# One core, a decoder layer on a hand-ordered TensorE stream: prepared blocks ahead of other late work, two closing products exchanged, the first quads' sums on VectorE, and a quarter of the k-tiles later where a stage begins

## The chip, the cores and the metric

The kernel runs on one core of a Trainium2 chip. The metric is the device time of one execution in microseconds (us), lower is better; a time is the median of several executions. The profile is one execution taken by the hardware profiler. Engines are named as in its rows: PE is TensorE (matmul), PEld its weight loads, DVE is VectorE, ACT is ScalarE, POOL is GpSimd, SP is SyncE, which issues most DMAs. L355 is line 355 of the kernel.

## The reference

One decoder layer on 256 tokens of width 2048 in float32: a half SwiGLU, a mixer, a second half SwiGLU, a final norm.

```python
x = x + 0.5 * swiglu(rmsnorm(x), ffn1_w_gate, ffn1_w_up, ffn1_w_down)      # 2048 -> 5632 -> 2048
x = x + hybrid_mixer(rmsnorm(x), w_in, ...)      # one projection w_in, attention, gated MLP, merge, w_out
x = x + 0.5 * swiglu(rmsnorm(x), ffn2_w_gate, ffn2_w_up, ffn2_w_down)
return rmsnorm(x, final_norm)

swiglu(h)       = (silu(h @ w_gate) * (h @ w_up)) @ w_down
hybrid_mixer(h) : proj = h @ w_in  -> q, k, v (3 x 1536), u, vs (1536), g_att, g_sg (2048)
                  y_att = attention(q, k, v) @ w_att_out;  y_sg = (gelu(u) * spatial(vs)) @ w_sg_out
                  merged = sigmoid(g_att) * y_att + sigmoid(g_sg) * y_sg;  return merged @ w_out
```

## The kernel before

All tokens stay in the core's memory; the weights stream through once. Every float32 product is made of three fp32r products: an operand is split into a high part (rounded, a copy by ACT) and a low part (the rest, a subtraction by DVE), and high x high, high x low and low x high are summed in PSUM. For the tokens these are `xhi`/`xlo` (h of the FFN: `hA`/`hB`; merged: `mhi`/`mlo`), for the weights `wh`/`wl`.

**Steps.** The work of PE is a list of steps (`steps`, made by `lay_out`). An ordinary step ("n") is two k-tiles of 128 rows by 512 columns of one weight; its unit `raw` is 512 KB, loaded by SP (L250), split by ACT (L348, `wh<-raw`) and DVE (L349, `wl<-raw`; all DVE instructions carry L66, a metering wrapper), and used by 12 matmuls (L355). `wh` and `wl` are rings of nine k-tiles. A function `advance` splits some three steps ahead of PE where the ring has room. A gemm has eight or fewer such steps (q = 0 to 7), one per two k-tiles.

**Quads.** For pairs of neighbouring gemms (512 columns each) some k-tiles are multiplied in Strassen's way, with seven block products p1 to p7 in place of eight: `nq` is 2 or 3 k-tile pairs (a row 128x1024 or 128x1536). The weight's four blocks B11, B21 (first gemm), B12, B22 (second) are loaded by `load_block` as `quads` (blocks 0 to 3). `prepare` makes from them f = B12+B22, t2 = f-B11, t1 = t2-B22, t4 = t2-B21, in this order (`todo`); p6 uses t2, p7 f, p5 t1, p4 t4. In rows `sum` or `part` is where t2 and t4 go, `quads` where f and t1 go. For the FFN quads f was made by the DMA itself: POOL loads block 3 onto block 2 with an accumulating DMA (L292). For the others DVE adds. Blocks of the next quad load when a product has freed their room (`FREES`: p5, p2, p7, p3). Token sums for the quads are `fx`, `fy`, `fh...`, `uTA`/`uTB`.

**Banks.** A quad has four PSUM banks: q11, q21 of its first gemm, q12, x_ of its second (`qd_0` to `qd_3` in rows). p1, p6, p7, p5 run in x_; after p5, DVE writes q12 = x_ + part (L414, a row `qd<-qd,quads`, `qd<-qd,part` or `qd<-qd,vs`), and from then on everything of the second gemm adds to q12 and x_. p3 goes to q12, p4 to q21, p2 to q11. `opening` puts p1, p6, p7 among the last steps of the gemms before, `closing` puts p5, p3, p4, p2 among the first steps of the quad's own.

**Order.** The first element of `group` is how many gemms are laid out together, the second a key that sorts their steps. `PAIR`, used where a stage's tokens come in quarters (four k-tiles each, c = 0 to 3), keeps the last two steps of both gemms (last quarter) for the end. It is used for the first pair of w_in, of w_out, of ffn2's gate, and of parts of the down product, which is cut into three parts (`PARTS`) of k-tiles as the FFN's columns get ready.

The rest is a planner at the time the program is built: `now[0]` is the step's time, `at(i, fn)` calls fn at a time, `extra(wait, slack, cost, fn)` puts work on a heap that `work_off` empties when the metered DVE load allows or the slack is over, `prepare_ready` prepares quads in `started` when their blocks are loaded, and `prepare_for` forces what a form about to be split needs. `move_in` loads the first four blocks of a home (a set of buffers for quads: two FFNs, gates, merge) at a given time. The engines then run their queues in program order, and semaphores do the rest.

Of the kernel before, what the change touches and what calls it, by code (L numbers as in the profile page):

```python
# [71 lines left out]
def layer(ctx: ExitStack, tc: tile.TileContext, a, out):  # L72
# [57 lines left out]
    quads = []  # L130
# [9 lines left out]
    slots = []  # L140

    def closing(count):
        return zip((1, 2, 3, 5) if count > 9 else (1, 2, 3, 4), ("p5", "p3", "p4", "p2"))

    def opening(count):
        return zip((5, 3, 1) if count > 9 else (4, 2, 1), ("p1", "p6", "p7"))
# [1 line left out]
    def lay_out():  # L148
        i, count = 0, 0
        while i < len(gemms):  # L150
            g = gemms[i]
            size, stage = g["group"]
            quad = g["quad"]
            taken = range(quad["k0"] // 2, quad["k0"] // 2 + quad["nq"]) if quad else ()
            order = [(p, q) for p in range(size) for q in range(gemms[i + p]["nk"] // 2) if q not in taken]
            if stage:
                order.sort(key=lambda s: stage(*s, gemms[i + s[0]]["nk"] // 2))
            new = [("n", (gemms[i + p], q // 2, q % 2)) for p, q in order]
            if quad:
                nq = quad["nq"]  # L160
                quad["gemms"] = gemms[i], gemms[i + 1]
                quad["loaded"], quad["split"] = {}, set()
                quad["todo"] = ["t2", "t1", "t4"] if quad["home"] in homes else ["f", "t2", "t1", "t4"]
                for k, form in opening(count):
                    steps.insert(len(steps) - k, ("s", (quad, form)))
                for k, form in reversed(list(closing(len(order)))):
                    new.insert(k, ("s", (quad, form)))
                quads.append(quad)
                for h in quad["gemms"]:
                    h["left"] = [3 * (h["nk"] - nq)] * NT  # L170
                gemms[i + 1]["left"][1] += 9 * nq
            steps.extend(new)
            count = len(order) if size > 1 else 16
            i += size
        t, pos = -1.0, 0
        for kind, s in steps:
            width = 2 if kind == "n" else s[0]["nq"]
            t += 1 if kind == "n" else width / 4
            ends.append(t)
            slots.append([(pos + q) % RING for q in range(width)])  # L180
            pos += width
            if kind == "n":
                hus.append(s)
                s[0]["steps"] += 1
            else:
                s[0]["gemms"][s[1] in ("p3", "p5", "p6", "p7", "p1")]["steps"] += 1
# [13 lines left out]
        return found  # L200


    PAIR = (2, lambda p, q, m: q >= m - 2)
    BOTH = (2, None)
    FIRST = (4, lambda p, q, m: 4 if q >= 4 else 3 if q >= 2 else 2 if p == 3 else q)

# [8 lines left out]

        heapq.heappush(extras, (now[0] + slack, next(counter), now[0] + wait, cost, fn))

    def work_off():
        DVE.load = max(0.0, DVE.load - TICK * (now[0] - now[1]))
        now[1] = now[0]  # L220
        while True:
            ready = [e for e in extras if e[2] <= now[0]]
            if not ready:
                return
            e = min(ready)
            if e[0] > now[0] and DVE.load + e[3] > FULL:
                return
            extras.remove(e)
            heapq.heapify(extras)
            e[4]()  # L230

    def start_of(w):
        return next(ends[i] - 1 for i, (kind, s) in enumerate(steps) if kind == "n" and s[0]["w"] is w)
# [52 lines left out]
    def load_block(quad, b):  # L286
        if quad is None:
            return
        quad["loaded"][b] = now[0]
        SP.dma_start(blocks_of(quad)[b], block(quad, b))  # L290
        if b == 2 and quad["home"] in homes:
            POOL.dma_start(blocks_of(quad)[b], block(quad, 3), accum_op=OP.add)  # L292

    def blocks_of(quad):
# [15 lines left out]
    def prepare_ready():  # L310
        for quad in started:
            if not quad["todo"]:
                continue
            what = quad["todo"][0]
            blocks, forms = NEEDS[what]
            if (all(quad["loaded"].get(b, 1e9) + 3 <= now[0] for b in blocks) and quad["split"].issuperset(forms)
                    and DVE.load + 0.56 * quad["nq"] * (NC / 512) <= FULL):
                assert all(b in quad["loaded"] for b in blocks)
                prepare_next(quad)
# [6 lines left out]
    started = []  # L326
# [10 lines left out]
    def split(i, k=None):  # L337
        kind, s = steps[i]
        if kind == "s":
            if s[1] == "p1":  # L340
                started.append(s[0])
            prepare_for(*s)
            s[0]["split"].add(s[1])
        r = raws[place[i]] if kind == "n" else form_of(*s)
        for first, end in runs(i, k or range(len(slots[i]))):
            o = slots[i][first]
            wh, wl = (v[:, o:o + end - first] for v in ring)
            ACT.activation(wh, r[:, first:end], AF.Copy)  # L348
            DVE.tensor_tensor(wl, r[:, first:end], wh.bitcast(F32), op=OP.subtract)  # L349
        if kind == "s" and s[1] in FREES:  # L350
            at(now[0] + (1 if s[1] == "p5" else 2), lambda: load_block(next_of(s[0]), FREES[s[1]]))
# [97 lines left out]
    def split_psum(hi, lo, src, slack=0):  # L449
        def rest():  # L450
            DVE.tensor_tensor(lo, src, hi.bitcast(F32), op=OP.subtract)

        ACT.activation(hi, src, AF.Copy)
        if slack:
            extra(1, slack, 1.1, rest)
        else:
            rest()
# [38 lines left out]
    def turned(ap):  # L496
        return ap.rearrange("p k (t i b) -> p (k t) i b", t=NT, b=32)
# [82 lines left out]
    homes = []  # L580
    merge = dict(make=merge_home)
    gates = dict(make=gate_home)

    def ffn(wg, wu, wd, down_post, group):
# [10 lines left out]
        for after, (part, quads_of) in zip(GATES, enumerate(PARTS)):  # L595
            for f in range(*after):
# [46 lines left out]
                quad = dict(k0=4 * CS[n], nq=2 if late else 3, forms=xT, home=merge if late else home)  # L643
                gemm(wg, f * NC, 0, KD, lhs_x, post_gate, BOTH if f else PAIR, bank, quad)
                gemm(wu, f * NC, 0, KD, lhs_x, post_up, BOTH, bank, quad)
            for c in range(4):
                if c % 2 == 0:
                    bank = side()
                    quad = dict(k0=quads_of["k0"], nq=quads_of["nq"], forms=sets[part], home=home)
                gemm(wd, c * NC, quads_of["f"][0] * NC, 4 * len(quads_of["f"]), lhs_h,  # L650
                     lambda e, banks, c=c, last=part == 2: down_post(e, c, banks, last), PAIR if c == 0 else BOTH,
                     bank, quad, quads_of["rooms"])
# [13 lines left out]
    mix = {}  # L666
# [343 lines left out]
    def post_merge(c):  # L1010
        def post(e, banks):
            post_mul("ga")(e, banks)
            ga, gs = mix["ga"], mix["gs"]
            if c == 0:
                mix["mhi"] = big.tile([P, KD, S], F32R, tag="E", name="mhi")
                mix["mlo"] = big.tile([P, KD, S], F32R, tag="C", name="mlo")

            def add():
                DVE.tensor_tensor(ga, ga, gs, op=OP.add)

            at(e + 1, add)

            def ev(src):
                split_psum(turned(mix["mhi"][:, 4 * c:4 * c + 4]), turned(mix["mlo"][:, 4 * c:4 * c + 4]), src)
                if c == CM:
                    sums_of(e + 10, mix, 0, 2, lambda: mix["fs"], src, "m", "tmp")

            turn(e + 2, f"m{c}", 8, put_tokens(lambda: ga), lambda: flat(ga), ev)
        return post

    front = [(o_s + j * NC, post_gelu("vs", j)) for j in range(3)] + [(o_u + j * NC, post_gelu("u", j)) for j in range(3)]
    for j, (c0, post) in enumerate(front):
# [3 lines left out]
        if j % 2 == 0:  # L1036
            bank = side()
            quad = dict(k0=4 * CS[1], nq=2, forms=xT, home=gates)
# [8 lines left out]
    for c in range(4):  # L1047
# [5 lines left out]
        else:  # L1053
            sides[0] += c == 2
            bank = side()
            quad = dict(k0=4 * CS[1], nq=2, forms=mix, home=merge)
# [4 lines left out]
    for c in range(4):  # L1061
        if c % 2 == 0:
            bank = side()
            quad = dict(k0=4 * CM, nq=2, forms=mix, home=merge)
        gemm(a["w_out"][0], c * NC, 0, KD, lambda: (mix["mhi"], mix["mlo"]),
             lambda e, banks, c=c: residual(e, 2, c, banks, 1.0, True), PAIR if c == 0 else BOTH, bank, quad)
# [52 lines left out]
    ffn2_gate = a["ffn2_w_gate"][0]  # L1119
# [9 lines left out]
    m = 0  # L1129
# [3 lines left out]
    mixer = start_of(w_in)  # L1133
# [3 lines left out]
    for h in range(2):  # L1137
        sgw_turn(mixer + 13 + 8 * h, h)
    at(ends[-1] - 36, load_fin)
    for after, home in ((16, homes[0]), (mixer + 5, gates), (start_of(ffn2_gate) + 3, homes[1])):  # L1140
        at(after, lambda home=home: move_in(home))


# [25 lines left out]
    b = tp_bank("gc0")  # L1169
# [28 lines left out]
    loaded, done = RAWB + MORE, 3  # L1198
# [26 lines left out]
    for i in range(n):  # L1225
        if i < n - LA - 1:
            products(i, jjs=(0,), high_first=i < 6)
            if i == 1:
                first_x((2, 3))
            if i == 3:  # L1230
                first_x(range(4, 8))
            products(i, jjs=(1,), high_first=i < 6)
        now[0] = ends[i]
        while callbacks and callbacks[0][0] <= ends[i]:
            heapq.heappop(callbacks)[2]()
        if i > 0:
            advance(i)
        for fn in after_splits:
            fn()
        after_splits.clear()  # L1240
        work_off()
        prepare_ready()
    for t in range(NT):
        known(t)
        for i in range(n - LA - 1, n):
# [51 lines left out]
```

## Time and profile before

| | |
|---|---|
| runs | 2014.84, 2018.8, 2019.36 us; median 2018.8 |
| profiled execution | 2018.7 us, span 2017.0 us, mean PE clock 0.994 |
| PE busy | 1984.2 us in 9188 matmuls |
| DVE, ACT busy | 1589.4, 1189.0 us |
| POOL busy | 57.1 us |
| DMA | 493.91 MB, mean 245 GB/s |

A busy share says little where one engine is at 98%: the reading goes by the idle stretches of PE, what ended each of them, and what the engine that ended it had been doing. PE's weight loads run beside its matmuls. A matmul row lasts 0.38 us while the next starts 0.216 us after it, because they are pipelined; so lost time shows between the starts of two rows.

### The profile page before, as it was taken

What the parts mean: (1) busy time and instruction counts of PE and PEld (TensorE: products, weight loads), DVE (VectorE), ACT (ScalarE), POOL (GpSimd) and SP (SyncE); (2) the same over time, 40 slices, a digit from 0 to 9 for tenths busy, and PEclk for the clock granted to TensorE, in tenths of its full rate; (3) what the DMA queues carried; (4) which work ended last, traced back from release to release, by engine and by line L of the source; (5) the groups of instructions that cost most, each with busy time, mean ns of one, the idle gap of its engine ahead of it and who ended that gap; (6) DMA issues with size and microseconds to landing.
All of it is one profiled execution on the core that took longest, in us unless ns stands there. A gap on an engine that the chain in (4) does not pass through costs nothing.

```text
span 2017.0 us, 25183 instructions
## 1 busy us (share of the span) xinstructions
PE 1984.2 (98%) x9188; PEld 1726.5 (86%) x9188; DVE 1589.4 (79%) x1652; ACT 1189.0 (59%) x1381; POOL 57.1 (3%) x50
## 2 busy tenths in 40 slices
PE   9999999999999999999999999989999999999998
PEld 8888888888888787888888888878888888888887
DVE  7698878888887687676665777886888788888886
ACT  7566556656666565455454555565665566555654
POOL 0000100000000000000000000000000000000000
PEclk9999999999999999999999999999999999999999
DMA  9798778787786975888887667768888778878883
GB/s 325 260 283 271 226 246 271 238 258 241 245 251 207 305 243 169 226 298 253 265 240 241 226 190 236 228 206 265 269 244 257 248 239 254 243 246 252 256 256 119
DMA packets 265444, 493.91 MB, mean 245 GB/s; under 512 B 17516, under 2 KB 46056, under 8 KB 265192
## 3 DMA queue, kind: packets, MB, share of 16 engines
q1 hardware_dynamic: 253624, 469.49, 71.6%
q0 software_dynamic: 11376, 22.28, 6.4%
q8 instruction: 72, 1.18, 0.2%
q10 hardware_dynamic: 320, 0.53, 0.1%
q14 instruction: 52, 0.43, 0.1%
HBM read 462.58 MB, written 29.66 MB: 244 GB/s over the span
## 4 chain that ended last, share of the span: by engine, by line
PE 86%; DVE 5%; DMA 4%; issue 2%; ACT 2%; SPq 0%; POOLq 0%; POOL 0%; ACTq 0%; DVEq 0%
PE qd L355 65%; PE mm L355 20%; DVE wl L66 3%; DMA raw<-in_w_in_dram 1%; DMA raw<-in_ffn_w_gate_dram 1%; ACT wh L348 1%; DMA raw<-in_ffn_w_up_dram 1%; DMA quads<-in_ffn_w_up_dram 0%; DMA bmu<-btu 0%; DVE vs L66 0%; DVE quads L66 0%; DVE sum L66 0%; ACT xt L566 0%; DMA xt<-bmx 0%; PE sp L802 0%
## 5 line engine op out<-in xcount | busy, mean ns | idle before, releaser
L66 DVE TENSOR_TENSOR wl<-raw,wh 128x1024 fp32r<-128x1024 f32 (+1 forms) x638 | 695.2, 1107 | 227.0 <-ACT wh L348 224.2
L348 ACT ACTIVATE wh<-raw 128x1024 fp32r<-128x1024 f32 (+1 forms) x638 | 609.0, 963 | 414.8 <-PE qd L355 236.9
L355 PE MATMUL qd<-wl,xhi 128*128 128x512 f32 x1201 | 456.2, 380 | 3.3 <-DVE wl L66 3.2
L355 PE MATMUL qd<-wh,xlo 128*128 128x512 f32 x1201 | 456.2, 380 | 2.0 <-DVE xlo L66 2.0
L355 PE MATMUL qd<-wh,xhi 128*128 128x512 f32 x1201 | 455.9, 380 | 0.0
L66 DVE TENSOR_TENSOR wl<-quads,wh 128x1536 fp32r<-128x1536 f32 (+2 forms) x222 | 289.6, 1319 | 142.6 <-ACT wh L348 141.6
L348 ACT ACTIVATE wh<-quads 128x1536 fp32r<-128x1536 f32 (+2 forms) x222 | 249.7, 1133 | 250.3 <-PE qd L355 236.9
L355 PEld LDWEIGHTS qd<-wl,xhi 128*128 128x128 f32 x1201 | 227.5, 189 | 36.5 <-DVE wl L66 4.1
L355 PEld LDWEIGHTS qd<-wh,xlo 128*128 128x128 f32 x1201 | 227.4, 189 | 35.2 <-DVE xlo L66 2.9
L355 PEld LDWEIGHTS qd<-wh,xhi 128*128 128x128 f32 x1201 | 227.6, 189 | 32.4
L355 PE MATMUL mm<-wh,xlo 128*128 128x512 f32 x608 | 232.0, 382 | 4.9 <-DVE xlo L66 4.9
L355 PE MATMUL mm<-wh,xhi 128*128 128x512 f32 x608 | 232.3, 382 | 0.2 <-ACT xhi L539 0.2
L355 PE MATMUL mm<-wl,xhi 128*128 128x512 f32 x608 | 229.7, 381 | 1.3 <-DVE wl L66 1.3
L355 PE MATMUL qd<-wl,hA 128*128 128x512 f32 x564 | 213.9, 379 | 0.6 <-DVE wl L66 0.6
L355 PE MATMUL qd<-wh,hA 128*128 128x512 f32 x564 | 213.8, 379 | 0.0
L355 PE MATMUL qd<-wh,hB 128*128 128x512 f32 x564 | 213.8, 379 | 0.0
L348 ACT ACTIVATE wh<-sum 128x1024 fp32r<-128x1024 f32 (+2 forms) x86 | 101.7, 1185 | 85.9 <-PE qd L355 70.5
L355 PEld LDWEIGHTS mm<-wh,xlo 128*128 128x128 f32 x608 | 115.6, 190 | 22.1 <-DVE xlo L66 5.6
L355 PEld LDWEIGHTS mm<-wl,xhi 128*128 128x128 f32 x608 | 115.7, 190 | 18.5 <-DVE wl L66 2.1
L355 PEld LDWEIGHTS mm<-wh,xhi 128*128 128x128 f32 x608 | 115.7, 190 | 16.6 <-ACT xhi L539 0.4
L355 PE MATMUL qd<-wh,fx 128*128 128x512 f32 x352 | 121.2, 385 | 8.4 <-DVE qd L66 5.3
L66 DVE TENSOR_TENSOR wl<-sum,wh 128x1024 fp32r<-128x1024 f32 (+2 forms) x86 | 117.5, 1375 | 10.3 <-ACT wh L348 10.3
(417 smaller groups left out, 2198.4 us busy)
## 6 DMA issues: line engine op xcount, KB each, us to landing
raw<-in_w_in_dram SPq DMA_DIRECT2D x168, 512.0 KB, 4.7
raw<-in_ffn_w_down_dram SPq DMA_DIRECT2D x120, 512.0 KB, 5.2
raw<-in_ffn_w_up_dram SPq DMA_DIRECT2D x112, 512.0 KB, 6.5
raw<-in_ffn_w_gate_dram SPq DMA_DIRECT2D x111, 512.0 KB, 3.9
quads<-in_ffn_w_gate_dram SPq DMA_DIRECT2D x38, 768.0 KB, 6.1
quads<-in_ffn_w_up_dram SPq DMA_DIRECT2D x38, 768.0 KB, 6.7
quads<-in_ffn_w_down_dram SPq DMA_DIRECT2D x32, 512.0 KB, 5.5
quads<-in_ffn_w_up_dram POOLq DMA_DIRECT2D x19, 768.0 KB, 10.8
```

Source lines behind the costliest of these rows:

```text
L66: return method(out, *args, **kwargs)
L348: ACT.activation(wh, r[:, first:end], AF.Copy)
L355: PE.matmul(g["ps"][t], act, in_turn(w), start=not g["begun"][t], stop=g["left"][t] == 0, skip_group_check=g["quad"] is not None)
```

## The change

- `closing`: p4 takes p3's position and p3 comes one position later.
- `PAIR` sorts in three groups and not two: the steps of the third quarter (the two before the last two) of both gemms come after the earlier ones of both.
- `quad["adds"]`: the accumulating DMA is kept only where the FFN home already had a quad; the first quad of either FFN has its f made by DVE from two plain loads.
- A quad enters `started` when its first block is loaded, no longer when p1 is split, and `prepare_ready` runs before `work_off`, with `settle` ahead of both.
- `mlo` of the first two quarters may wait (`extra`), and the second FFN's `move_in` is two steps earlier.

```diff
     def closing(count):
-        return zip((1, 2, 3, 5) if count > 9 else (1, 2, 3, 4), ("p5", "p3", "p4", "p2"))
+        return zip((1, 2, 4, 5) if count > 9 else (1, 2, 3, 4), ("p5", "p4", "p3", "p2"))
...
-                quad["todo"] = ["t2", "t1", "t4"] if quad["home"] in homes else ["f", "t2", "t1", "t4"]
+                quad["adds"] = quad["home"] in homes and any(q["home"] is quad["home"] for q in quads)
+                quad["todo"] = ["t2", "t1", "t4"] if quad["adds"] else ["f", "t2", "t1", "t4"]
...
-    PAIR = (2, lambda p, q, m: q >= m - 2)
+    PAIR = (2, lambda p, q, m: 2 if q >= m - 2 else q >= m - 4)
...
-    def work_off():
+    def settle():
         DVE.load = max(0.0, DVE.load - TICK * (now[0] - now[1]))
         now[1] = now[0]
+
+    def work_off():
...
     def load_block(quad, b):
         if quad is None:
             return
+        if not quad["loaded"]:
+            started.append(quad)
         quad["loaded"][b] = now[0]
         SP.dma_start(blocks_of(quad)[b], block(quad, b))
-        if b == 2 and quad["home"] in homes:
+        if b == 2 and quad["adds"]:
             POOL.dma_start(blocks_of(quad)[b], block(quad, 3), accum_op=OP.add)
...
         if kind == "s":
-            if s[1] == "p1":
-                started.append(s[0])
             prepare_for(*s)
...
-                split_psum(turned(mix["mhi"][:, 4 * c:4 * c + 4]), turned(mix["mlo"][:, 4 * c:4 * c + 4]), src)
+                split_psum(turned(mix["mhi"][:, 4 * c:4 * c + 4]), turned(mix["mlo"][:, 4 * c:4 * c + 4]), src, c < 2)
...
-    for after, home in ((16, homes[0]), (mixer + 5, gates), (start_of(ffn2_gate) + 3, homes[1])):
+    for after, home in ((16, homes[0]), (mixer + 5, gates), (start_of(ffn2_gate) + 1, homes[1])):
...
-        work_off()
+        settle()
         prepare_ready()
+        work_off()
```

The numbers of matmuls and of SP's DMAs stay; DVE has two additions of 128x1536 more, POOL two DMAs fewer. How the rows move, at three places:

*First part of the first FFN's down product (place K).* PE before: the quad's p5 (`fh23` into bank `qd_3`) is followed by a step of the first gemm (banks `qd_0`, `qd_1`), and p3 into `qd_2` comes after it.

```order
L355 MATMUL qd_3_1294<-wl,fh23.0_845 128x512
L355 MATMUL qd_3_1294<-wh,fh23.0_845 128x512
L355 MATMUL qd_0_1291<-wh,hA 128x512
L355 MATMUL qd_0_1291<-wl,hA 128x512
L355 MATMUL qd_0_1291<-wh,hB 128x512
L355 MATMUL qd_1_1292<-wh,hA 128x512
```

PE after, from the same row on:

```order
L358 MATMUL qd_3_1293<-wl,fh23.0_845 128x512
L358 MATMUL qd_3_1293<-wh,fh23.0_845 128x512
L358 MATMUL qd_2_1292<-wh,hA 128x512
L358 MATMUL qd_2_1292<-wl,hA 128x512
L358 MATMUL qd_2_1292<-wh,hB 128x512
L358 MATMUL qd_3_1293<-wh,hA 128x512
```

A step of the second gemm, on banks `qd_2` and `qd_3`, now follows p5. DVE at the same place, before (`bth` is the turning of the FFN's products, the row of `qd_2` is L414's):

```order
L66 STREAM_TRANSPOSE bth63.75_1436<-sg56.5_1286 128x4x4x32 x2
L66 TENSOR_TENSOR wl<-quads,wh 128x1536
L66 TENSOR_TENSOR wl<-raw_1327,wh 128x1024
L66 TENSOR_TENSOR qd_2_1293<-qd_3_1294,quads 128x512
L66 TENSOR_TENSOR wl<-sum,wh 128x1536
```

and after:

```order
L66 STREAM_TRANSPOSE bth63.75_1436<-sg56.5_1284 128x4x4x32 x2
L66 TENSOR_TENSOR wl<-sum,wh 128x1536
L66 TENSOR_TENSOR wl<-raw_1327,wh 128x1024
L66 TENSOR_TENSOR wl<-raw_1353,wh 128x1024
L66 TENSOR_TENSOR qd_2_1292<-qd_3_1293,quads 128x512
```

One more subtraction for the weights stands ahead of L414's row.

*w_out, around the last quarter of `mlo`.* DVE before (`quads<-quads,part` is f, `sum<-quads` t2, `quads<-sum,part` t1, `sum<-quads,sum` t4):

```order
L66 TENSOR_TENSOR wl<-quads,wh 128x1024
L66 TENSOR_TENSOR quads<-quads,part 128x1024
L66 TENSOR_TENSOR wl<-raw_9168,wh 128x1024
L66 TENSOR_TENSOR sum<-quads 128x1024
L66 TENSOR_TENSOR wl<-raw_9199,wh 128x1024
L66 TENSOR_TENSOR quads<-sum,part 128x1024
L66 TENSOR_TENSOR wl<-sum,wh 128x1024
L66 TENSOR_TENSOR wl<-raw_9215,wh 128x1024
L66 TENSOR_TENSOR sum<-quads,sum 128x1024
L66 TENSOR_TENSOR mlo<-ga458.75_8964,mhi 128x1024
```

and after:

```order
L66 TENSOR_TENSOR wl<-quads,wh 128x1024
L66 TENSOR_TENSOR wl<-raw_9170,wh 128x1024
L66 TENSOR_TENSOR wl<-raw_9192,wh 128x1024
L66 TENSOR_TENSOR quads<-quads,part 128x1024
L66 TENSOR_TENSOR sum<-quads 128x1024
L66 TENSOR_TENSOR wl<-sum,wh 128x1024
L66 TENSOR_TENSOR quads<-sum,part 128x1024
L66 TENSOR_TENSOR wl<-raw_9216,wh 128x1024
L66 TENSOR_TENSOR sum<-quads,sum 128x1024
L66 TENSOR_TENSOR mlo<-ga458.75_8967,mhi 128x1024
```

The same rows, but f and t2 stand behind both subtractions for raw units.

*Start of the second FFN.* SP before (`bmx` and `xt` carry the last quarter of x through DRAM to turn it; `quads` are the first blocks):

```order
L250 DMA raw_9764<-in_ffn_w_up_dram 128x2x512
L250 DMA raw_9795<-in_ffn_w_up_dram 128x2x512
L468 DMA bmx_3_9815<-btx_3_9812 128x1024
L290 DMA quads<-in_ffn_w_gate_dram 128x3x512
L290 DMA quads<-in_ffn_w_up_dram 128x3x512 x2
L290 DMA quads<-in_ffn_w_gate_dram 128x3x512
L250 DMA raw_9838<-in_ffn_w_gate_dram 128x2x512
```

and after:

```order
L253 DMA raw_9766<-in_ffn_w_up_dram 128x2x512
L295 DMA quads<-in_ffn_w_gate_dram 128x3x512
L295 DMA quads<-in_ffn_w_up_dram 128x3x512 x2
L295 DMA quads<-in_ffn_w_gate_dram 128x3x512
L253 DMA raw_9806<-in_ffn_w_up_dram 128x2x512
L471 DMA bmx_3_9826<-btx_3_9823 128x1024
L253 DMA raw_9828<-in_ffn_w_gate_dram 128x2x512
```

The four loads of the quad went ahead of a raw unit and of the store `bmx_3`.

More of the change, by code (lines that the diff above doesn't have):

```diff
@@ L1240, in layer @@
         after_splits.clear()
+        settle()
+        prepare_ready()
         work_off()
-        prepare_ready()
     for t in range(NT):
```

## The prediction

> **What bounds the kernel now.** I read the page first: busy time of each engine, then the chain that ended last.
>
> ```profile
> PE 1984.2 (98%) x9188; PEld 1726.5 (86%) x9188; DVE 1589.4 (79%) x1652; ACT 1189.0 (59%) x1381; POOL 57.1 (3%) x50
> PE 86%; DVE 5%; DMA 4%; issue 2%; ACT 2%; SPq 0%; POOLq 0%; POOL 0%; ACTq 0%; DVEq 0%
> ```
>
> TensorE is the bound: 98% busy, and 86% of the chain. No matmul is added or removed, so the change can only move the places where TensorE stands still. The view of waits names them for the product lines, as total, times, longest:
>
> ```profile
> PE qd L355 <- DVE qd L66: 6.3, 6, 3.8
> PE mm L355 <- DVE xlo L66: 4.9, 1, 4.9
> PE qd L355 <- DVE wl L66: 4.3, 3, 3.2
> PE qd L355 <- DVE xlo L66: 2.0, 2, 1.4
> ```
>
> Then TensorE's timeline (start, duration, group, and in brackets the idle time before it with what ended it):
>
> ```profile
> 80.47 0.48 PE L355 MATMUL mm<-wl,xhi 128*128 128x512 f32 x1 [1.01 <-DVE wl L66]
> ...
> 103.88 0.38 PE L355 MATMUL qd<-wl,xhi 128*128 128x512 f32 x1
> 104.10 0.38 PE L355 MATMUL qd<-wh,xlo 128*128 128x512 f32 x1
> 104.59 0.45 PE L355 MATMUL qd<-wh,fx 128*128 128x512 f32 x1
> ...
> 684.20 0.80 PE L355 MATMUL mm<-wh,xlo 128*128 128x512 f32 x1 [4.88 <-DVE xlo L66]
> ...
> 772.54 0.77 PE L355 MATMUL qd<-wh,fx 128*128 128x512 f32 x1 [3.80 <-DVE qd L66]
> ...
> 1287.53 0.48 PE L355 MATMUL qd<-wh,mlo 128*128 128x512 f32 x1 [1.06 <-DVE mlo L66]
> ...
> 1334.68 0.48 PE L355 MATMUL qd<-wh,fx 128*128 128x512 f32 x1 [2.29 <-ACT qd L407]
> ...
> 1355.62 0.45 PE L355 MATMUL qd<-wh,fx 128*128 128x512 f32 x1 [1.15 <-DVE qd L66]
> ...
> 1379.72 0.74 PE L355 MATMUL qd<-wl,xhi 128*128 128x512 f32 x1 [3.21 <-DVE wl L66]
> ...
> 1937.14 0.38 PE L355 MATMUL qd<-wh,hB 128*128 128x512 f32 x1
> 1937.62 0.45 PE L355 MATMUL qd<-wh,fh691.0_13449 128*128 128x512 f32 x1
> ...
> 1978.86 0.45 PE L355 MATMUL qd<-wh,fh691.0_13449 128*128 128x512 f32 x1 [0.85 <-DVE qd L66]
> ```
>
> Matmuls start 0.216 us apart (103.88 to 104.10), so an ordinary step of 12 takes 2.59 us. I count a loss from start to start: the step from 104.10 to 104.59 loses 0.28, which the idle column does not show. The longest idles are followed by a second loss, in the granted clock (stretch, TensorE busy, others, PEclk, DMA share):
>
> ```profile
> 683.49:690.32 6.83, 6.12 (x14) 4.87 (x15) 3.32 (x6) 1.06 (x1) 1.10 (x1) 0.50 0.93 326
> 772.24:775.65 3.41, 3.11 (x7) 2.52 (x8) 1.64 (x3) 1.46 (x2) 0.00 (x0) 0.50 0.28 76
> 1335.44:1338.85 3.41, 3.41 (x10) 2.65 (x9) 3.37 (x5) 3.38 (x9) 0.00 (x0) 0.50 0.39 136
> 1379.81:1383.23 3.42, 3.42 (x8) 2.72 (x9) 3.42 (x4) 3.39 (x5) 0.00 (x0) 0.50 0.51 163
> ```
>
> After each of the four idles of 2.29 us and more TensorE ran 3.4 us, once 6.8, at clock 0.50: about half of that, 1.5 to 1.8 us, or 3.1, is lost on top. After the idles of 1.15 and less it did not. All losses of the trace together are some 38 us of 2017; the change cannot win more.
>
> **The change, part by part.** Plus is time won.
>
> *Closing order p5, p4, p3, p2.* p3 writes bank q12, which VectorE fills first (L414, q12 = x_ + part, after p5). At twelve quads p3 waits 0.10 to 0.33 us for that, from 104.10 to 1937.14, in sum 3.0; the first interval after is 0.07 longer each time (104.59 to 104.88), so 3.8. With p3 two or three steps later they go. Two of the twelve belong to the places K below, leaving +3.1. The same wait at 1978.86 is worth +1.1, and that at 1355.62 +1.3. There the xlo of 1.4 us (waits) also goes, since two "up" steps now come before gate's q4: another +1.7, together +3.0 (0 to 3.0).
>
> The dear one, before 772.54, is 3.97 and 1.6 of half clock, 5.57. VectorE was late:
>
> ```profile
> 771.70 0.69 DVE L66 TENSOR_TENSOR qd<-qd,vs 128x512 f32<-128x512 f32 x1
> ```
>
> p4 stands there now. But this quad's block 3 loads later (p3 frees its room), so f, t2 and t1 move later into a stretch where VectorE has no gaps; two of them at 1.22 (as the mlo row below, same shape) make its wl late by about 2.5. I take two thirds of that for a new stall, 1.65: +3.9, between 0 (the wait comes back whole) and 5.6.
>
> *Later f and t2, also in w_out.* Before, mlo of the last quarter came just after its use:
>
> ```profile
> 1278.31 1.06 ACT L348 ACTIVATE wh<-raw 128x1024 fp32r<-128x1024 f32 x1 [0.89 <-PE qd L355]
> ...
> 1280.06 1.22 DVE L66 TENSOR_TENSOR wl<-raw,wh 128x1024 fp32r<-128x1024 f32 x1
> ...
> 1286.26 1.22 DVE L66 TENSOR_TENSOR mlo<-ga458.75_8964,mhi 128x1024 fp32r<-128x1024 f32 x1
> ```
>
> In the new order f comes behind the wl of that wh (the second row), which can start at 1279.4: wl to 1280.5, then f, t2, wl, t1, wl, t4, mlo, seven at 1.13 to 1.22 with a wait for one wh, ending about 1289.7 and not 1287.5. The stall of 1.2 becomes 3.5, long enough for a half clock of 1.6: -3.9 (-1 to -5.5).
>
> *Third quarter later (PAIR).* In the mixer's first pair TensorE does 6656's first four units and not 6144's q4, q5 at 678.94, so the 5.04 and 3.1 before and after 684.20 go, +8.15. But the next quarter's rows stand where they stood, since DMA sets them (share 0.93 in the window above):
>
> ```profile
> 697.92 1.72 ACT L566 ACTIVATE xt<-xt,gcols 128x256 f32<-128x256 f32 x4 [0.72 <-DMA xt<-bmx]
> ...
> 700.63 1.99 ACT L348 ACTIVATE wh<-raw 128x1024 fp32r<-128x1024 f32 x2
> ...
> 701.90 1.22 DVE L66 TENSOR_TENSOR wl<-raw,wh 128x1024 fp32r<-128x1024 f32 x1
> ```
>
> ScalarE does these in order, so the wl of step 299 still ends at 703.1, and TensorE, 8.15 earlier, is there at 698.2: idle 4.9, with 1.9 of half clock. Net +1.3 (0 to 8.15).
>
> In the first down part of both FFNs (place K) the same rule puts the second product's first step right behind p5. It writes q12 and x_ itself, so it waits for L414, as p3 did a step later. VectorE was already full there:
>
> ```profile
> 180.31 1.72 DVE L66 TENSOR_TENSOR wl<-quads,wh 128x1536 fp32r<-128x1536 f32 x1
> 181.95 1.21 DVE L66 TENSOR_TENSOR wl<-raw,wh 128x1024 fp32r<-128x1024 f32 x1
> 183.08 0.69 DVE L66 TENSOR_TENSOR qd<-qd,quads 128x512 f32<-128x512 f32 x1
> ...
> 1522.16 1.21 DVE L66 TENSOR_TENSOR wl<-raw,wh 128x1024 fp32r<-128x1024 f32 x1
> 1523.29 0.69 DVE L66 TENSOR_TENSOR qd<-qd,quads 128x512 f32<-128x512 f32 x1
> ...
> 183.44 0.38 PE L355 MATMUL qd<-wh,hB 128*128 128x512 f32 x1
> 183.92 0.45 PE L355 MATMUL qd<-wh,fh23.0_845 128*128 128x512 f32 x1
> ```
>
> The new order has one more wl (1.13) ahead of the qd row, so it ends at 184.9 and not 183.77. p5 ended a step before 183.66, at 181.07. TensorE stands 181.07 to 185.0, 3.95, where it lost 0.33: -3.6, and in the second FFN (1521.2 to 1525.2) the same. Both idles are as long as that before 772.54, so half clock, 1.6 to 3.1; I take 1.9 each: -11.0 (-5.0 if the clock stays and the order eases, -13.5). The third down part, where p5 is followed by one more step of the first product, costs 0.25 each: -0.5.
>
> *First quad's sum by VectorE, move_in two steps earlier.* Two POOL accumulate DMAs go, two 128x1536 additions of 1.75 come. In the first FFN VectorE has idle time for it; the rows that landed late behind the accumulate land earlier and the wl before 80.47 is in time: +1.2 (0 to 1.2). In the second:
>
> ```profile
> 1358.94 8.03 DMA quads<-in_ffn_w_up_dram
> ...
> 1377.31 1.76 DVE L66 TENSOR_TENSOR sum<-quads 128x1536 f32<-128x1536 f32 x1 [6.12 <-DMA quads<-in_ffn_w_up_dram]
> ...
> 1378.64 1.71 ACT L566 ACTIVATE xt<-xt,gcols 128x256 f32<-128x256 f32 x4 [5.78 <-DMA xt<-bmx]
> ```
>
> The first row is of the chain: a block was issued at 1358.94 and took 8.03. t2 (sum<-quads) waited 6.12 for the accumulate behind it. On SP the four blocks now go ahead of one raw load and the store bmx2_3. They can go when w_out's last matmul has freed their room, about 1347, and at 8.03 each land by about 1361, when VectorE reaches f; xt lands some 9 us earlier. On POOL only rstd stood behind the accumulate. The 3.37 before 1379.72 and 1.8 of half clock go: +5.2 (-7 to +5.2). What is late next there is TensorE itself.
>
> *Preparation ahead of extras, mlo's slack:* same instructions in another order, in places with gaps: 0.
>
> Sum: 3.1 + 1.1 + 3.0 + 3.9 - 3.9 + 1.3 - 11.0 - 0.5 + 1.2 + 5.2 = +3.4. From the profiled execution, 2018.7 (span 2017.0 and 1.7 around it; the median of the runs is 2018.8): 2015.3.
>
> The Trainium skill weighs in on the half clock. "TensorE: Matmul & The Clock Gate", Part 1, says that the clock halves only after a whole idle window of about 3.4 us, windows running free. The trace differs: 2.29 us before 1334.68 was enough. By the rule the idles at K and in w_out would mostly go unpunished, and the sum would be the first rival's.
>
> **Rivals.**
> 1. The clock stays at the moved waits (3.5 at w_out, twice 3.95, 4.9): 1.6 + 3.8 + 1.9 come back, +10.7, 2008. Against it: four of four idles from 2.29 on were followed by 0.50.
> 2. The next quarter in the mixer comes with TensorE, because its loads are issued earlier when the pair's order changes: +8.15 for +1.3, 2008.5. For it: its loads wait in SP's queue; against: DMA share 0.93.
> 3. A wait comes back where it was: the late f, t2 and t1 cost the gates' quad all of the 3.9, or K gets the 6.8 us window (3.1 for 1.9, twice): the sum is -0.5 or +1.0, 2018 to 2019, no change. For it: VectorE's stretches at both places show no gap.
> 4. Slower: f holds VectorE's queue in the second FFN. Every wl behind f waits for the blocks, and they share the DMA with the raw loads. Ten us late is ten less the 4.6 by which a wl is done ahead (1281.3 by the 1280.06 row, its step began at 1285.9, two matmuls before the idle of 1287.53), and 1.8 of half clock: -7.2 for +5.2, 2027.7. It decides from about 5 us late (a landing at 1366.5), where the half clock sets in. Against it: 8.03 is the time on a full DMA already.
>
> **How the numbers follow.** A measurement here tells 0.2%, 4 us, from none: under 2014.8 is faster, over 2022.8 slower. My sum, 0.36, lies at the border (half of it on each side); rivals 1 and 2 together 0.27; rival 3, 0.26; rival 4, 0.11. So faster 0.18 + 0.27, rounded to 0.46; same 0.18 + 0.26, 0.43; slower 0.11. The range leaves out rival 4 and the two gains together: 2004 to 2022.
>
> **What would show it.** Right: no idle before the first matmul after 678.94, nor at the old 772.5 and 1379.7; a new one of about 4 us behind p5 in both first down parts, ended by DVE qd, with PEclk 0.50 after; 3 to 4 us at mlo; two accumulate DMAs fewer. Wrong: no wait at K, or a wait of "quads<-quads" on DMA in the second FFN.

## The result, and the profile after

The changed kernel took 2012.55 us in the median of 20 runs (2008.47 to 2017.4), the kernel before 2018.05 in as many: ratio 0.9974, 95% interval 0.9966 to 0.9982. That is 5.5 us faster, 0.26%, where 3.4 were forecast. The profiled execution took 2012.44, its span is 2010.7, 6.3 less than before. The page's busy times and chain:

```profile
PE 1981.1 (99%) x9188; PEld 1732.3 (86%) x9188; DVE 1594.0 (79%) x1655; ACT 1188.5 (59%) x1382; POOL 52.5 (3%) x48
PE 91%; DVE 3%; DMA 2%; issue 2%; ACT 2%; SPq 0%; POOLq 0%; POOL 0%; ACTq 0%; DVEq 0%
```

The same matmuls, two POOL instructions fewer, and PE's share of the chain up from 86 to 91%. The view of waits shows that the waits did not vanish but changed their owners:

```profile
PE qd L358 <- DVE qd L66: 7.5, 2, 3.8
PE qd L358 <- DVE mlo L66: 2.7, 1, 2.7
PE mm L358 <- ACT wh L351: 2.3, 1, 2.3
...
PE qd L358 <- DVE vs L66: 1.7, 1, 1.7
```

The sum q12 (row one) cost 6.3 at six places; it now costs 7.5 at two. PE's timeline has the idles, with place K at 183.97 and 1515.67:

```profile
183.97 0.48 PE L358 MATMUL qd<-wh,hA 128*128 128x512 f32 x1 [3.73 <-DVE qd L66]
...
704.85 0.48 PE L358 MATMUL mm<-wh,xhi 128*128 128x512 f32 x1 [2.28 <-ACT wh L351]
...
768.51 0.48 PE L358 MATMUL qd<-wh,fx 128*128 128x512 f32 x1 [1.67 <-DVE vs L66]
...
1286.93 0.80 PE L358 MATMUL qd<-wh,mlo 128*128 128x512 f32 x1 [2.70 <-DVE mlo L66]
...
1515.67 0.79 PE L358 MATMUL qd<-wh,hA 128*128 128x512 f32 x1 [3.80 <-DVE qd L66]
```

Neither the idle before the old 684.20 nor that of 1379.72 has a successor of its size. VectorE's timeline answers for place K and for the second FFN's start:

```profile
180.95 2.35 DVE L66 TENSOR_TENSOR wl<-raw,wh 128x1024 fp32r<-128x1024 f32 x2
183.22 0.69 DVE L66 TENSOR_TENSOR qd<-qd,quads 128x512 f32<-128x512 f32 x1
...
1360.11 1.75 DVE L66 TENSOR_TENSOR quads<-quads 128x1536 f32<-128x1536 f32 x1
...
1366.82 1.75 DVE L66 TENSOR_TENSOR sum<-quads 128x1536 f32<-128x1536 f32 x1
```

Two subtractions for raw units, not one, stand ahead of q12's sum (second row, x2). f (third row) and t2 (fourth) have no bracket: VectorE waited for no block there, where t2 waited 6.12 before.

### The profile page after: what moved, and what is told of

It is laid out like the page before. It is cut to its first block, busy times and chain, and to the rows that moved or that the text cites. A ratio compares the mean times of both kernels' runs of the same rounds, so it can differ in the third digit from the quotient of the medians.

```text
span 2010.7 us, 25179 instructions
## 1 busy us (share of the span) xinstructions
PE 1981.1 (99%) x9188; PEld 1732.3 (86%) x9188; DVE 1594.0 (79%) x1655; ACT 1188.5 (59%) x1382; POOL 52.5 (3%) x48
## 4 chain that ended last, share of the span: by engine, by line
PE 91%; DVE 3%; DMA 2%; issue 2%; ACT 2%; SPq 0%; POOLq 0%; POOL 0%; ACTq 0%; DVEq 0%
PE qd L358 68%; PE mm L358 22%; DVE wl L66 2%; DMA xt<-bmx 1%; ACT wh L351 1%; ACT xt L569 0%; DMA raw<-in_w_in_dram 0%; DVE quads L66 0%; DVE sum L66 0%; DMA part<-in_ffn_w_up_dram 0%; PE sp L805 0%; PE warm L1169 0%; DVE vs L66 0%; SPq L477 0%; PE pv L980 0%
## 5 line engine op out<-in xcount | busy, mean ns | idle before, releaser
L358 PEld LDWEIGHTS qd<-wh,hA 128*128 128x128 f32 x564 | 107.6, 191 | 23.5 <-DVE qd L66 8.3
```

The lines of the kernel that those rows point to most:

```text
L358: PE.matmul(g["ps"][t], act, in_turn(w), start=not g["begun"][t], stop=g["left"][t] == 0, skip_group_check=g["quad"] is not None)
```

## The experiments

Losses below are counted between the starts of matmuls, beyond 0.216 us each, with the half clock that follows; they hold to some 0.1 us. Ratios are to the kernel before, measured beside each run (2017.66 to 2018.11 us).

**e1: the old sorting key in the down products.**

```diff
     PAIR = (2, lambda p, q, m: 2 if q >= m - 2 else q >= m - 4)
+    LAST = (2, lambda p, q, m: q >= m - 2)
...
-    ... down_post(e, c, banks, last), PAIR if c == 0 else BOTH,
+    ... down_post(e, c, banks, last), LAST if c == 0 else BOTH,
```

> The changed kernel, but the down products keep the old sorting key of two groups; the mixer and the second FFN's gate keep the new one. Theory (the loss at place K is the price of putting a second-gemm step behind p5): the two stretches from 179.86 and 1511.49 in the changed kernel's profile, 5.6 us each with their half clock, go, and the clock is 1.00 there; 2012.5 - 11 = 2001.5, 0.9918 of before. Rival (TensorE only waits there for VectorE's backlog, which it meets a few steps later anyway): the idle moves to p4 or p3 of the same quad, ended by DVE wl, at 2 us or more each, and the time is 2006 or more.

Measured: 1999.39, ratio 0.9909 (0.9896 to 0.9922). The stretches of place K in both FFNs, by the view of windows (us, PE busy, PEld, DVE, ACT, POOL, PEclk, DMA share, GB/s):

```profile
178.00:190.00 12.00, 12.00 (x57) 10.53 (x56) 8.80 (x10) 6.58 (x7) 0.00 (x0) 1.00 0.96 267
1500.00:1515.00 15.00, 15.00 (x71) 13.15 (x70) 11.81 (x14) 8.03 (x8) 0.97 (x1) 1.00 0.94 244
```

PE is busy throughout at clock 1.00, so the rival's later wait does not exist. VectorE's order there is the same as in the changed kernel; only the step behind p5 differs. The place of that step is what K costs: 11.2 us in the rows (5.64 and 5.60). The medians differ by 13.2; another 1.7 is at the mixer's start, where the wait of the changed kernel's trace (5.46) comes without a half clock (3.8).

**e2: q12's sum ahead of the subtractions.** The changed kernel with

```diff
+        if steps[i][0] == "s" and steps[i][1][1] == "p5":
+            for fn in after_splits:
+                fn()
+            after_splits.clear()
         if i > 0:
             advance(i)
```

> The changed kernel, but after p5 VectorE's sum q12 = x_ + part is issued ahead of the weight subtractions that are issued at the same step, and not behind them. Theory: at place K it comes right behind the 128x1536 wl, so it ends at 181.6 and not 183.9; TensorE idles 1.6 us there, too little for a half clock, and the loss is 1.6 each and not 5.6: 2004.5, 0.9933. Rival (VectorE's whole load decides, not its order): the subtractions that are now later make TensorE wait one or two steps later, and it is 2010 or more.

Measured: 2005.25, ratio 0.9936 (0.9924 to 0.9949). VectorE's and PE's timelines at K:

```profile
180.74 0.69 DVE L66 TENSOR_TENSOR qd<-qd,quads 128x512 f32<-128x512 f32 x1
181.34 2.34 DVE L66 TENSOR_TENSOR wl<-raw,wh 128x1024 fp32r<-128x1024 f32 x2
...
181.49 0.48 PE L358 MATMUL qd<-wh,hA 128*128 128x512 f32 x1 [1.47 <-DVE qd L66]
```

The sum comes first, the idle is 1.47 and no half clock follows; the losses are 1.73 and 1.80. Order in VectorE's queue, not its load, sets this wait.

**e3: only the exchange of p3 and p4**, in the kernel before (the one line of `closing`).

> The kernel before with p3 and p4 exchanged and nothing else. Theory: the ten small waits at p3 (0.10 to 0.33, in sum 3.0), 1.0 at 1978.86, 1.3 at 1355.62 and 3.1 of the 5.6 at 772.54 go; the late f and t2 in w_out cost 4.0 at mlo; in sum -4.4: 2013.6, 0.9978, with a wait of 2.7 us or more for mlo. Rival (the late f and t2 at mlo come from preparing ahead of extras or from the later start in PAIR): no longer wait at mlo, 2009.5, 0.9958.

Measured: 2013.95, ratio 0.998 (0.9971 to 0.9988), the theory's time. PE's waits:

```profile
PE qd L355 <- DVE wl L66: 5.4, 3, 3.6
PE qd L355 <- DVE xlo L66: 5.1, 2, 3.6
PE mm L355 <- DVE xlo L66: 4.9, 1, 4.9
PE qd L355 <- DVE mlo L66: 2.7, 1, 2.7
```

No row for q12 is left, and the wait for mlo is there without any other edit: the exchange makes f and t2 of w_out late. Not all terms came as the theory had them. A wait for xlo in the second FFN grew from 1.4 to 3.6, with a half clock, so that the stretch of 1345 to 1362 loses 7.2 where it lost 4.0; the changed kernel's other edits remove it.

**e4: only the first quads' sums and the earlier move_in** (with the start of a quad at its first load), in the kernel before.

> The kernel before with the first quads' f on VectorE, the quads started at their first load, and the second FFN's first blocks loaded two steps earlier; nothing else. Theory: the 1.3 us at 80.47 and the 5.2 at 1379.72 go, 2011.6, 0.9968; no wait longer than 1 us between 1360 and 1385. Rival (the gain needs the other edits, since f then holds up VectorE's queue): TensorE waits between 1360 and 1385 for a wl, 2016 or more.

Measured: 2012.89, ratio 0.9975 (0.9967 to 0.9984). The second FFN's start by windows:

```profile
1360.00:1376.00 16.00, 16.00 (x76) 14.02 (x75) 12.20 (x11) 9.58 (x13) 1.00 (x1) 1.00 0.76 251
1376.00:1385.00 9.00, 9.00 (x44) 7.87 (x43) 9.00 (x9) 5.98 (x8) 0.00 (x0) 1.00 0.50 152
```

PE never stops there. These edits alone are worth 5.2 us by the medians, nearly as much as the whole change; f does not hold up the queue. What the sums and the earlier loads are worth singly was not tried.

**e6: the old sorting key everywhere**, in the changed kernel.

> The changed kernel with the old sorting key everywhere, in the down products, the mixer's first pair and the second FFN's gate. Against e1 (1999.4) it tells what the key is worth where it does no harm. Theory: at the mixer's start the wait for xlo with its half clock comes back, 8.15 for the 3.8 that e1 loses between 675 and 710, and the one for xlo in the second FFN, 1.7: 2005.5, 0.9938. Rival (the prediction's term: the wait only moves to the next quarter, worth 1.3, and the second FFN's xlo is in time anyway): 2000.7, 0.9914.

Measured: 2008.07, ratio 0.9951 (0.9939 to 0.9964), on the theory's side and beyond it. PE's timeline:

```profile
683.14 0.79 PE L358 MATMUL mm<-wh,xlo 128*128 128x512 f32 x1 [4.95 <-DVE xlo L66]
...
1354.27 0.48 PE L358 MATMUL qd<-wh,xlo 128*128 128x512 f32 x1 [2.78 <-DVE xlo L66]
```

Both waits for xlo are back. Between 675 and 710 e6 loses 7.5 and e1 3.8; from 1320 to 1360 it loses 10.0 and e1 5.1. So the key is worth some 8.6 us at the mixer and the gate, and cost more than that in the down products.

**e7: the heap's work ahead of the preparation**, as before, in the changed kernel (`work_off()` and `prepare_ready()` swapped).

> The changed kernel, but the work on the heap is emptied ahead of the preparation of quads at each step, as before; quads still start at their first load. Theory (the order between them falls in places with gaps): no difference from the changed kernel, 2012.5 within 1.5, and no place loses or gains over 0.5 us. Rival (preparing ahead is what keeps t1 and t4 in time now that block 3 is loaded later): new waits ended by DVE wl at p4 or p5, 2015 or more.

Measured: 2014.62, ratio 0.9986 (0.9977 to 0.9995); its profiled execution took 2012.29, the changed kernel's 2012.44. Its places lose what the changed kernel's do, but for the half clock (below) and one new wait for q12's sum, 0.89 at 1352.84, more than the 0.5 that the theory allowed. The changed kernel, run again, has a new wait of its own near there (0.93 at 1341.69), so one trace of each does not tell whether the order made it. Whether the order is worth the 2 us between the medians stays open: the intervals overlap.

**e8: p3 and p4 in their old order**, in the changed kernel.

> The changed kernel with p3 and p4 in their old order. Theory: the small waits come back (3.0), and 1.0 in the last down part, 3.1 at the gates' quad, 1.3 in the second FFN; the wait for mlo falls by 4.0; at place K VectorE has one subtraction fewer ahead of q12, so the idle is 2.8 and not 3.9, 1.1 less twice: 2012.5 + 8.4 - 6.2 = 2014.7, 0.9983. Rival (at K it is p3 or the second gemm alike that waits, and the half clock hides the difference): no less at K, 2017.

Measured: 2017.21, ratio 0.9997 (0.9987 to 1.0007). At K, with one subtraction fewer ahead of q12's sum:

```profile
183.11 0.80 PE L358 MATMUL qd<-wh,hA 128*128 128x512 f32 x1 [2.60 <-DVE qd L66]
...
1512.57 0.48 PE L358 MATMUL qd<-wh,hA 128*128 128x512 f32 x1 [2.67 <-DVE qd L66]
```

The idles are 1.1 less, as the theory said, yet the time is the rival's. The profiled execution took 2011.78 and the runs spread to 2023; they had less luck with the half clock, or lose elsewhere, which the one profile cannot tell. At any rate the whole change without the exchange is no gain, and the exchange is worth about 5 us in it.

**e5: e1, with the old closing order for all quads of the merge buffers**, to win the wait for mlo back.

```diff
-    def closing(count):
+    def closing(count, quad):
+        if quad["home"] is merge:
+            return zip((1, 2, 3, 5) if count > 9 else (1, 2, 3, 4), ("p5", "p3", "p4", "p2"))
```

> The kernel of e1 (old sorting key in the down products), and the quads of the mixer's gates, merge and w_out that live in the merge buffers keep the old closing order p5, p3, p4, p2. Theory (the wait for mlo near 1276.5 in e1, 2.86 and its half clock, comes from f and t2 of the w_out quad, which the exchange makes late): it shrinks to the 1.2 of the kernel before without a half clock, -4.1, and three waits of 0.23 at p3 come back, +0.7: 1996.0, 0.9891. Rival (mlo is late because VectorE's queue is full there in any order): the wait stays at 2.5 or more, and the time is 2000 or more.

Measured: 2000.27, ratio 0.9916 (0.9902 to 0.993): the theory was right on the place and wrong on the time. PE's timeline:

```profile
1279.02 0.48 PE L361 MATMUL qd<-wh,mlo 128*128 128x512 f32 x1 [1.06 <-DVE mlo L66]
...
1317.14 0.48 PE L361 MATMUL qd<-wh,xlo 128*128 128x512 f32 x1 [0.65 <-DVE xlo L66]
...
1341.12 0.48 PE L361 MATMUL qd<-wh,fx 128*128 128x512 f32 x1 [1.04 <-DVE part L66]
```

The wait for mlo is 1.06 again, but from 1315 to 1347 it loses 8.1 where e1 lost 5.0, and the mixer 4.3 for 2.9, with a half clock.

**e9: e5, with the readings after p5 and p7 ahead of the splits** (e2's edit with `in ("p5", "p7")`).

> The kernel of e5, and after p5 and p7 the reading of bank x_ (VectorE's q12 = x_ + part and part - x_, ScalarE's q21 = x_) is issued ahead of the splits of that step. Theory (order in VectorE's queue at these places costs what the rows say, 1.14 per subtraction): the wait for part at the gates' quad, 1.83, falls to 0.7, and that of 0.9 in the second FFN's first quad goes: 1994, 0.9881. Rival (a reading that waits for TensorE holds up the splits behind it): waits for wl appear after p5 or p7, and it is 1997 or more.

Measured: 2001.13, ratio 0.9916 (0.9903 to 0.993). The wait at the gates' quad is 0.70 where it was 1.83, as the row said, but no time was won; it is the rival's (1997 or more), and the waits for wl, its sign, rose from 2.7 to 4.6 in sum. The longest wait of all is another:

```profile
PE mm L361 <- ACT wh L354: 3.1, 1, 3.1
```

That is the mixer's next quarter (1.28 before it in e5). PE came there some 0.6 us earlier (a wait of 1.38 at 653.54 for one of 2.01), and the quarter, which goes through DRAM, was not in time for it. What else made it late, and why waits for wl of 2.1 appeared at 1318, was not tried.

**e10: e1, with the old closing order for w_out's first quad alone.** That quad's p3 frees the room of the next one's block 3.

```diff
+        if quad["gemms"][0]["w"] is w_out and quad["gemms"][0]["c0"] == 0:
+            return zip((1, 2, 3, 5) if count > 9 else (1, 2, 3, 4), ("p5", "p3", "p4", "p2"))
```

> The kernel of e1, and the first quad of w_out alone keeps the old closing order, so that block 3 of the next one loads as early as before. Theory (e5 took the wait for mlo away, and lost it again because the later quads of the merge buffers, those of the second FFN's start above all, got the old order too): the loss near 1276 falls from 5.5 to 1.3, one wait of 0.23 at p3 comes back, and the stretch from 1315 to 1345 stays at e1's 5.0: 1995.5, 0.9888. Rival (f and t2 made early push TensorE's waits into the start of the second FFN whatever quad they belong to): 7 or more between 1315 and 1350, 1999 or more.

Measured: 1997.54, ratio 0.9899 (0.9883 to 0.9915). Waits of PE:

```profile
PE qd L361 <- ACT qd L413: 2.3, 1, 2.3
PE qd L361 <- DVE wl L66: 2.1, 2, 1.8
PE qd L361 <- DVE vs L66: 1.7, 1, 1.7
PE mm L361 <- DVE wl L66: 1.2, 2, 1.0
PE qd L361 <- DVE mlo L66: 1.1, 1, 1.1
```

It loses 1.33 near 1276 and 5.3 from 1315 to 1345: the theory, with 2 us less than it said. This is the best version, 20 us under the kernel before. Its interval and e1's overlap, so the step from e1 is shown by the rows (1276: 5.48 to 1.33) rather than by the times.

**after_again: the changed kernel, beside e8 and e10.**

> The changed kernel once more, beside e10 and e8 on the same chip, and for the clock at place K. Theory (half a window of idle and a bit halves the next one: in all traces so far a window of the 3.413 us grid with 2.04 us of idle or more was followed by clock 0.50, one with 1.99 or less was not): every window here with 2.04 or more is followed by 0.50 and none with less, 2012.5. Rival (the length of the idle decides, wherever the grid lies): an idle of 2.3 or more without a half clock does not occur.

Measured: 2011.86, ratio 0.9973 (0.9963 to 0.9984), which repeats the result. On the clock, see the last section.

## Why the prediction was right, point by point

The sum was +3.4, measured 5.5 by the medians and 6.3 between the two profiles. By its terms, predicted and found in the rows before and after:

| term | predicted | found |
|---|---|---|
| small waits at p3, without K | +3.1 | +2.4 and the first intervals, all gone |
| last down part (1978.86) | +1.1 | +1.0 |
| gates' quad (772.54) | +3.9 | +3.1 (5.57 to 2.47) |
| second FFN's start, 1323 to 1359 | +3.0 | +5.2 (10.33 to 5.09) |
| mlo in w_out | -3.9 | -4.0 (1.33 to 5.37) |
| mixer's first pair | +1.3 | +2.7 (8.15 to 5.46) |
| place K, twice | -11.0 | -10.7 (0.26, 0.33 to 5.64, 5.60) |
| third down part | -0.5 | 0, no loss there |
| first quad, 80.47 | +1.2 | +1.3 |
| second FFN's quad, 1379.72 | +5.2 | +5.2 |
| unpriced: end of the first FFN, near 655 | 0 | -1.0 (0.85 to 1.89) |
| unpriced: a wait for wl near 865 | 0 | +0.5 |

The found terms make 5.7; the rest of the 6.3 are intervals too small to place. Each is from one trace before and one after, and a half clock that comes or stays away moves a term by 1.7 or more.

- K came out to a few tenths: one more subtraction ahead of q12's sum, an idle of 3.9 ended by it, and 1.7 of half clock. e1 and e2 show the cause by taking away the step and the order.
- The mlo term too, though 0.8 of it is a wait for `mhi` ahead (ACT, at 1283.53) that was not named: e3 shows that the exchange alone makes the term, e10 that one quad's closing order does.
- The sums on VectorE: e4 shows them together with the earlier loads and no other edit, 5.2 us by the medians, PE without a stop from 1360 to 1385. The last block landed at 1361.0, as worked out, and rival 4 has no support.
- The gates' quad came near by its size and not by its cause. The stall of 1.65 was to be a late wl. The 1.83 found are at p5, where TensorE waits for VectorE's reading of p7 (`vs<-vs,qd` at 767.78, DVE vs); e9 moves that reading ahead of the splits, and the wait falls to 0.70.
- Mis-sized was the mixer. I had the new wait at 4.9 of idle; it was 3.7 (2.44 and 1.23). In e1 it is 2.4 and without a half clock, so the next quarter does come a little earlier, as rival 2 had it, though not by its 6.9.
- Mis-sized was also the second FFN's start. I left the waits of 0.29, 0.92 and 0.71 between 1323 and 1330 at nothing; they went. The 0.92 is in e8, which lacks the exchange, and not in e1, so the exchange removes it; that a later f and t2 leave VectorE free for xlo there is likely and not shown.
- Not seen at all was the loss near 655. It is 1.80 in e3 and 0.89 in e8, so the exchange costs 1 us there; by which row was not tried.
- Rival 1 (the clock stays) did not happen in the profiled execution, where all four moved waits (idles of 3.73, 2.28 and 0.96 together, 2.70, 3.80) were followed by a clock of 0.50. In the second run it happened at one K and at the mixer, in e7 at one K. Of rival 3, 2.5 of the gates' quad's 5.57 came back, not all; but its long half clock at K, 6.8 us, is in e7 (1513.28 to 1520.11) and in the second run (183.38 to 190.21).
- Of the edits costed at nothing, the order of preparation and heap shows one place that moved by 0.89 (e7); that and the 2 us between the medians leave it open. The slack of `mlo` was taken back only together with others (e4).

The two largest terms, K and the second FFN's quad, rest on waits that the experiments take away, and they hold within 0.3. That the small rest came out at all near the forecast is partly luck: the errors of the terms go from -1.0 to +2.2 and come to +2.3 (5.7 for 3.4), two thirds of the forecast, and the trace after is one in which the clock fell at every moved wait, as the sum had it. One slip in the working hangs on nothing: the chances add up to 0.45 and 0.44 where it has 0.46 and 0.43.

## What to carry to other kernels

When a step is moved behind another, look at which bank it writes and who must fill that bank first: a sorting key that helped at two places (8.6 us) cost 11 at two others, where it set a reader of a fresh sum right behind its maker. Undo such an edit place by place, not as a whole: the change was worth 5.5 us, without the key in the down products 18.7 (e1), and with one quad's closing order put back as well 20 (e10). And a gain ahead of a transfer that sets a date of its own (the mixer's next quarter in e9) is given back there.

## What the runs showed of the hardware that was not expected

The half clock goes by a free-running grid of 3.413 us, and what counts is the idle time within one window of it. The starts and ends of all half-clock periods of one execution lie a whole number of such windows apart (before: from 683.49 to 772.24 it is 26.0, on to 1335.44 165.0, on to 1379.81 13.0). With the grid laid through them, and the idle of a window taken as what PE's busy time leaves of it, windows at full clock with 2.0 us or more of idle were followed by a clock of 0.50 and those with 1.80 or less by 1.00, in all 13 traces. Between, both occurred: 1.82 in e3 (from 1278.52) was followed by 0.50, 1.95 in the changed kernel's second run (from 1514.57, below) was not. So the limits of 2.04 and 1.99 in that run's theory are too sharp for all the traces, though no window of that run breaks them. A window at half clock was followed by full clock where it had 0.6 us of idle or less, by another half one where it had 0.65 or more (the last row below; 0.70 in the first of the two from 683.49 to 690.32 before). So an idle of the same length can cost nothing, 1.7 us, or twice that. The idles of 3.73 and 3.80 us at place K in e7, first and second FFN, by windows of its grid:

```profile
178.67:182.08 3.41, 1.47 (x7) 0.94 (x5) 3.41 (x5) 2.11 (x2) 0.00 (x0) 1.00 1.02 223
182.08:185.50 3.42, 1.63 (x8) 1.45 (x9) 1.74 (x2) 0.00 (x0) 0.00 (x0) 1.00 1.08 283
185.50:188.91 3.41, 3.41 (x17) 3.01 (x16) 1.06 (x1) 1.78 (x3) 0.00 (x0) 1.00 1.07 369
...
1509.87:1513.28 3.41, 0.55 (x3) 0.15 (x1) 3.41 (x3) 1.41 (x2) 0.00 (x0) 1.00 1.05 199
1513.28:1516.70 3.42, 2.48 (x6) 2.03 (x7) 0.89 (x2) 0.00 (x0) 0.00 (x0) 0.50 1.05 326
1516.70:1520.11 3.41, 3.41 (x10) 2.69 (x9) 0.69 (x1) 0.63 (x1) 0.00 (x0) 0.50 1.05 306
```

In the first FFN the grid cut the idle in two (1.94 and 1.79), and the clock stayed; in the second 2.86 fell into one window and 0.94 into the next, and two windows ran at 0.50. In the changed kernel run again it was the other way round:

```profile
1511.16:1514.57 3.41, 1.55 (x8) 1.01 (x6) 3.41 (x4) 2.11 (x2) 0.00 (x0) 1.00 1.01 216
1514.57:1517.98 3.41, 1.46 (x7) 1.30 (x8) 1.89 (x3) 0.00 (x0) 0.00 (x0) 1.00 1.08 290
...
179.96:183.37 3.41, 0.33 (x2) 0.00 (x0) 3.41 (x4) 1.18 (x2) 0.00 (x0) 1.00 1.08 207
183.37:186.78 3.41, 2.76 (x7) 2.22 (x8) 0.59 (x1) 0.00 (x0) 0.00 (x0) 0.50 1.05 348
```

The idle of 3.81 us at the second K (1.86 and 1.95 in its two windows) cost no clock, so the rival of that run (length decides) falls. The Trainium skill, "TensorE: Matmul & The Clock Gate", Part 1, has the window and that it runs free, and the traces agree; that a whole window must be idle they contradict: some 2 us of it are enough. That a kernel's times spread by this is argued, not shown: e1's four runs lie within 1 us (1999.28 to 2000.28) with two half clocks in its trace, the changed kernel's twenty within 9 with five; but e10's four spread over 6 (1994.66 to 2000.6), and its trace has one.
